# Weight buffers moved by 96 bytes against x and the activated tiles

## The chip, the cores and the metric

One Trainium2 chip, one core. The time is device microseconds of one execution of the whole kernel. A core has five engines that run side by side: TensorE (PE, with its weight loads shown as PEld), VectorE (DVE), ScalarE (ACT), GpSimd (POOL) and SyncE (SP, which issues most transfers). SBUF is the on-chip memory of 128 partitions; an address below is a byte offset within each partition.

## The reference

One inference step of a one-layer decoder trunk on 256 prompt tokens and 8 x 4 sample tokens (288 in all, width 2048). Each sub-layer stands between two RMS norms:

```
x = x + 0.5 * norm1(swiglu(norm0(x), ffn1_w_in, ffn1_w_out))      # hidden width 5632
x = x + norm3(hybrid_mixer(norm2(x), mix_w_in, ..., mix_w_out))   # two groups of gated linear recurrences
x = x + 0.5 * norm5(swiglu(norm4(x), ffn2_w_in, ffn2_w_out))

def swiglu(x, w_in, w_out):
    gate, up = split(x @ w_in, 2)
    return (silu(gate) * up) @ w_out
```

All is float32. Outputs are x for prompt and sample and the new recurrent states.

## The kernel before

Activations are kept transposed: the 2048 features as 16 tiles of 128 partitions x 288 tokens. To keep float32 accuracy with one-pass matmuls, each operand is split into a high part (rounded to the matmul's float32r) and a low part (what is left). A product of a weight block and an activation tile is three matmuls into the same PSUM tile, high x high, high x low and low x high (lines 615 to 617). The weights are the stationary operand, loaded anew before each matmul, and the 288 tokens stream past:

```
yield lambda: PE.matmul(dst, w[0][:, a, c], parts[0], ...)   # L615: high weights, high x
yield lambda: PE.matmul(dst, w[0][:, a, c], parts[1], ...)   # L616: high weights, low x
yield lambda: PE.matmul(dst, w[1][:, a, c], parts[0], ...)   # L617: low weights, high x
```

Weights arrive in units of 256 x 512 numbers (two k tiles, four column blocks of 128). `Weights.load` has SP fetch one into a raw tile (3 buffers of 4096 bytes); `Weights.pieces` splits it: ACT writes the high half (L119), DVE the low half (L120) of a tile `wh` of 8192 bytes, in which each of the two k tiles has 512 high numbers and behind them 512 low ones. `wh` has 4 buffers in the pool hlp, and for about a third of the units around each border between sub-layers 2 extra buffers in a pool hx on the right side of SBUF. Every unit feeds 24 matmuls. `block` walks over units, column blocks and k tiles; the order is that of the code.

The high and low parts of an activation tile lie in one tile of 2304 bytes. `pair` allots it as four places of 576 bytes; each place holds 72 high numbers, then 72 low ones, so a low part starts 288 bytes behind its high part. A matmul reads 4 numbers (16 bytes) from each of the four places in turn, then the next 4 (`turns_of`):

```
PLACES, LINE = 4, 4
t = pool.tile([P, PLACES, 2, T // PLACES], F32R, name=name)
return t[:, :, 0, :], t[:, :, 1, :]
def turns_of(t):
    return t.rearrange("p g (i e) -> p i g e", e=LINE)
```

Such tiles are xp (x, 16 tiles), fill x and y (4 + 4 tiles at each border, in a pool `fl`), and hp (the activated hidden tiles silu(gate) * up, 2 buffers in the pool ffn, each four tiles in the same layout).

Pools on the left of SBUF are stacked upward in the order in which they are opened: const, xpool (x, y, xp, rt, rp, acc, cols), rawp, hlp (the four wh), sqp, colp, then the pools of the sub-layer (ffn1, mixer or ffn2). Pools on the right are stacked downward: a pool `top` with a gap of 224 bytes, hx below it, fl below that. Within a pool the first tile has the lowest address. Before the change, modulo 128: every wh is at 0, the high part of every xp, hp and fill tile at 64, the low part at 64 + 288 = 96. So wh stands 64 bytes past a high part and 32 past a low part, in all products.

Of the kernel before, what the change touches and what calls it, by code (L numbers as in the profile page):

```python
# [9 lines left out]
F32 = mybir.dt.float32  # L10
# [6 lines left out]
P = 128  # L17
# [31 lines left out]
def pair(pool, name):  # L49

    t = pool.tile([P, PLACES, 2, T // PLACES], F32R, name=name)
    return t[:, :, 0, :], t[:, :, 1, :]
# [97 lines left out]
def trunk_kernel(ctx, tc, x_prompt, x_sample, state_gla, state_hgrn, norm_gains, f1_in, f1_out, f2_in, f2_out,  # L150
# [6 lines left out]
    xpool = ctx.enter_context(tc.tile_pool(name="xpool", bufs=1))  # L157
    rawp = ctx.enter_context(tc.tile_pool(name="rawp", bufs=RAW_BUFS))
    hlp = ctx.enter_context(tc.tile_pool(name="hlp", bufs=HL_BUFS))
    mmp = ctx.enter_context(tc.tile_pool(name="mmp", bufs=5, space=PSUM))  # L160
    aux = ctx.enter_context(tc.tile_pool(name="aux", bufs=3, space=PSUM))
    sqp = ctx.enter_context(tc.tile_pool(name="sqp", bufs=2))
# [63 lines left out]
    def wider(n):  # L226

        return {i for i in range(n - 44, n + 4) if i // 2 % 3 == (n + 2) // 2 % 3}
# [268 lines left out]
    class PreNorm:  # L497
# [3 lines left out]
        def __init__(self, name, update, ahead, at):  # L501

            self.name, self.update, self.ahead, self.at, self.late = name, update, ahead, at, []
            self.tmps = None
# [25 lines left out]
    class Fill:  # L530
# [2 lines left out]

        def __init__(self, pool, name, gains, gnext, some, ahead):
            self.gnext, self.name, self.some, self.ahead = gnext, name, some, ahead

            self.tiles = [[pair(pool, f"{name}{n}{k}") for k in range(EARLY)] for n in "xy"]
            self.gains = pool.tile([P, 48], F32, name=f"{name}g")[:, 0:EARLY]
            V.tensor_tensor(self.gains, gains[:, 0:EARLY], prm[:, gnext * KT:gnext * KT + EARLY], op=ALU.mult)
# [138 lines left out]
    def ffn(tag, gcol, gnext, pn, before, fill=None):  # L678
# [2 lines left out]
        border = []  # L681
        with ExitStack() as pools:
            fp = pools.enter_context(tc.tile_pool(name=f"ffn{tag}", bufs=2))
            hid, final_tiles = {}, []

            def do_in(c):
# [1008 lines left out]
    class Border:  # L1695


        def __init__(self, n, gains, gnext, some, ahead=0):
            self.pools = ExitStack()
            top = self.pools.enter_context(tc.tile_pool(name=f"top{gnext}", bufs=1, side="right"))  # L1700
            top.tile([P, 56], F32, name=f"gap{gnext}")
            W.begin_extra(self.pools.enter_context(tc.tile_pool(name=f"hx{gnext}", bufs=2, side="right")), wider(n))
            self.fill = Fill(self.pools.enter_context(tc.tile_pool(name=f"fl{gnext}", bufs=1, side="right")),
                             f"fill{gnext}", gains, gnext, some, ahead)

    pn = pre1 = PreNorm("pre1", x_first, FIRST, 11)
    pn.late.append(prm2)
    u, border = ffn(1, lambda k: hg1[:, k:k + 1], 2, pn, first)
    u, border = mixer(PreNorm("pre2", u, UPDATED, 11), border)
    ffn(2, lambda k: hg1[:, KT + k:KT + k + 1], None, PreNorm("pre3", u, UPDATED, 11), border.pools, border.fill)  # L1710


# [39 lines left out]
```

## Time and profile before

| | |
|---|---|
| runs | median 2184.03 us (2183.36 to 2198.98) of 3 |
| profiled execution | 2185.01 us, span 2183.2 us, granted TensorE clock 0.999 |
| TensorE matmuls | 17828, busy 2174.0 us |
| weight loads | 17828, busy 2155.0 us |
| VectorE, ScalarE | busy 1384.0 and 1018.5 us |
| read from HBM | 363.75 MB, 172 GB/s with what is written |

The span is the time from the first to the last instruction. Matmuls are pipelined: one is recorded as some 290 ns long, while the next starts after about 130 ns. So the distance from start to start is what a matmul costs, and it is got by counting records in a window of time.

### The profile page before, as it was taken

The numbers are of one execution on the slowest core, as the hardware profiler recorded it, in microseconds if no ns is written. First come the engines' busy times: TensorE is split into PE (matmuls) and PEld (weight loads), VectorE is DVE, ScalarE is ACT, GpSimd is POOL, SyncE is SP. The second block draws the span as 40 slices with busy tenths as digits, with TensorE's granted clock in tenths as the row PEclk, the third lists the DMA queues.
The fourth block names the chain that finished last, engine by engine and source line by source line (L and its number), as shares of the span: only waits on it lengthen the run. The fifth ranks groups of instructions, "written<-read, shape, count | busy, mean of one in ns | idle before, by whom it ended". The sixth has DMA issues, their size and how long they took to land.

```text
span 2183.2 us, 43224 instructions
## 1 busy us (share of the span) xinstructions
PE 2174.0 (100%) x17828; PEld 2155.0 (99%) x17828; DVE 1384.0 (63%) x2253; ACT 1018.5 (47%) x1537; POOL 180.0 (8%) x327
## 2 busy tenths in 40 slices
PE   9999999999999999999999999999999999999999
PEld 9999999999999999999999999999999999999998
DVE  7655546554656468888898756745555466556656
ACT  6453434343334346665677654543334343433344
POOL 2000000000000001323300000000000020122005
PEclk9999999999999999999999999999999999999999
DMA  7655555555556554677665664655655565666555
GB/s 220 182 173 173 173 174 172 174 173 174 174 174 192 167 172 136 202 214 207 178 187 170 183 195 126 181 167 164 175 173 167 172 178 175 177 179 184 167 168 160
DMA packets 227335, 384.87 MB, mean 176 GB/s; under 512 B 21363, under 2 KB 60865, under 8 KB 227137
## 3 DMA queue, kind: packets, MB, share of 16 engines
q1 hardware_dynamic: 213872, 365.02, 56.1%
q0 software_dynamic: 10992, 16.77, 2.8%
q8 instruction: 140, 2.29, 0.4%
q10 hardware_dynamic: 2272, 0.31, 0.1%
q14 instruction: 59, 0.48, 0.1%
HBM read 363.75 MB, written 11.80 MB: 172 GB/s over the span
## 4 chain that ended last, share of the span: by engine, by line
PE 92%; DVE 3%; DMA 2%; ACT 1%; issue 1%; SPq 0%; POOL 0%; ACTq 0%; DVEq 0%; POOLq 0%
PE gate L616 10%; PE gate L615 9%; PE gate L617 9%; PE out L616 8%; PE out L615 8%; PE up L616 8%; PE out L617 8%; PE up L615 8%; PE up L617 8%; PE mo L616 2%; PE mo L615 2%; PE mo L617 2%; PE hfq L615 1%; PE hfq L616 1%; PE hfq L617 1%; DVE wh L120 1%
## 5 line engine op out<-in xcount | busy, mean ns | idle before, releaser
L120 DVE TENSOR_TENSOR wh<-raw,wh 128x1024 fp32r<-128x1024 f32 (+1 forms) x676 | 821.6, 1217 | 597.5 <-ACT wh L119 595.8
L119 ACT ACTIVATE wh<-raw 128x1024 fp32r<-128x1024 f32 (+1 forms) x676 | 710.3, 1052 | 923.9 <-PE gate L617 289.0
L615 PE MATMUL gate<-xp,wh 128*128 128x288 f32 x1660 | 481.9, 292 | 0.2
L616 PE MATMUL gate<-xp,wh 128*128 128x288 f32 x1660 | 480.8, 292 | 0.5 <-DVE xp L282 0.4
L617 PE MATMUL gate<-xp,wh 128*128 128x288 f32 x1660 | 477.9, 289 | 0.0
L616 PE MATMUL out<-hp,wh 128*128 128x288 f32 x1408 | 410.6, 292 | 0.0
L616 PE MATMUL up<-xp,wh 128*128 128x288 f32 x1408 | 410.5, 292 | 0.0
L615 PE MATMUL out<-hp,wh 128*128 128x288 f32 x1408 | 409.0, 290 | 0.3 <-DVE y L801 0.3
L615 PE MATMUL up<-xp,wh 128*128 128x288 f32 x1408 | 408.9, 290 | 0.0
L617 PE MATMUL out<-hp,wh 128*128 128x288 f32 x1408 | 407.6, 289 | 0.0
L617 PE MATMUL up<-xp,wh 128*128 128x288 f32 x1408 | 407.1, 289 | 0.0
L615 PEld LDWEIGHTS gate<-xp,wh 128*128 128x128 f32 x1660 | 311.2, 188 | 1.1 <-issue 0.3
L616 PEld LDWEIGHTS gate<-xp,wh 128*128 128x128 f32 x1660 | 310.2, 188 | 1.6 <-DVE xp L282 1.3
L617 PEld LDWEIGHTS gate<-xp,wh 128*128 128x128 f32 x1660 | 311.1, 188 | 0.2 <-DVE wh L120 0.2
L615 PEld LDWEIGHTS out<-hp,wh 128*128 128x128 f32 x1408 | 264.6, 188 | 0.6 <-DVE y L801 0.5
L615 PEld LDWEIGHTS up<-xp,wh 128*128 128x128 f32 x1408 | 264.3, 188 | 0.0
L617 PEld LDWEIGHTS up<-xp,wh 128*128 128x128 f32 x1408 | 264.2, 188 | 0.1
L617 PEld LDWEIGHTS out<-hp,wh 128*128 128x128 f32 x1408 | 264.3, 188 | 0.0
L616 PEld LDWEIGHTS out<-hp,wh 128*128 128x128 f32 x1408 | 264.0, 188 | 0.0
L616 PEld LDWEIGHTS up<-xp,wh 128*128 128x128 f32 x1408 | 264.0, 188 | 0.0
L801 DVE TENSOR_TENSOR y<-out,y 128x288 f32<-128x288 f32 x287 | 119.7, 452 | 79.2 <-PE out L617 78.7
L758 POOL DMA_DIRECT2D xT<-b x64 | 37.1, 586 | 754.8 <-PE gate L617 564.8
(417 smaller groups left out, 2549.0 us busy)
## 6 DMA issues: line engine op xcount, KB each, us to landing
raw<-in_ffn_w_in_dram SPq DMA_DIRECT2D x350, 512.0 KB, 3.7
raw<-in_ffn_w_out_dram SPq DMA_DIRECT2D x176, 512.0 KB, 3.6
raw<-in_mix_w_in_dram SPq DMA_DIRECT2D x64, 512.0 KB, 4.3
raw<-in_mix_w_in_dram SPq DMA_DIRECT2D x96, 256.0 KB, 3.4
raw<-in_mix_w_out_dram SPq DMA_DIRECT2D x32, 512.0 KB, 3.7
out_dram<-s POOLq DMA_DIRECT2D x32, 256.0 KB, 2.9
s<-in_state_gla_dram SPq DMA_DIRECT2D x16, 256.0 KB, 5.6
s<-in_state_hgrn_dram SPq DMA_DIRECT2D x16, 256.0 KB, 5.6
```

Of the source, the lines that this page charges most:

```text
L119: i1 = self.nc.scalar.activation(h[:, a, c], raw[:, a, c], AF.Copy).ins
L120: i2 = self.nc.vector.tensor_tensor(l[:, a, c], raw[:, a, c], h[:, a, c].bitcast(F32), op=ALU.subtract).ins
L615: yield lambda: PE.matmul(dst, w[0][:, a, c], parts[0], start=start, stop=False)
L616: yield lambda: PE.matmul(dst, w[0][:, a, c], parts[1], start=False, stop=False)
L617: yield lambda: PE.matmul(dst, w[1][:, a, c], parts[0], start=False, stop=stop)
L758: queues[n % len(queues)].dma_start(dst[q * TS:(q + 1) * TS, 4 * g:4 * g + 4, :, cols].rearrange("p k t c -> p (k t) c"), b32[rows, q])
L801: V.tensor_tensor(y[k], ps, y[k], op=ALU.add)
```

## The change

Three gaps are added and one is made larger; nothing else is changed. A tile that is only allotted takes space and no time.

```
     hlp = ctx.enter_context(tc.tile_pool(name="hlp", bufs=HL_BUFS))
+    hlp.tile([P, 24], F32, name="gap_w", bufs=1)
...
         def __init__(self, pool, name, gains, gnext, some, ahead):      # class Fill
             self.gnext, self.name, self.some, self.ahead = gnext, name, some, ahead
+            pool.tile([P, 24], F32, name=f"{name}gap")
...
             fp = pools.enter_context(tc.tile_pool(name=f"ffn{tag}", bufs=2))
+            fp.tile([P, 8], F32, name=f"gap_f{tag}", bufs=1)
...
             top = self.pools.enter_context(tc.tile_pool(name=f"top{gnext}", bufs=1, side="right"))
-            top.tile([P, 56], F32, name=f"gap{gnext}")
+            top.tile([P, 64], F32, name=f"gap{gnext}")
```

The line numbers 615 to 617 become 617 to 619, and 119 and 120 stay.

More of the change, by code (lines that the diff above doesn't have):

```diff
@@ L159, in trunk_kernel @@
     hlp = ctx.enter_context(tc.tile_pool(name="hlp", bufs=HL_BUFS))
+    hlp.tile([P, 24], F32, name="gap_w", bufs=1)
     mmp = ctx.enter_context(tc.tile_pool(name="mmp", bufs=5, space=PSUM))
@@ L535, in __init__ @@
             self.gnext, self.name, self.some, self.ahead = gnext, name, some, ahead
+            pool.tile([P, 24], F32, name=f"{name}gap")
             self.tiles = [[pair(pool, f"{name}{n}{k}") for k in range(EARLY)] for n in "xy"]
@@ L683, in ffn @@
             fp = pools.enter_context(tc.tile_pool(name=f"ffn{tag}", bufs=2))
+            fp.tile([P, 8], F32, name=f"gap_f{tag}", bufs=1)
             hid, final_tiles = {}, []
@@ L1700, in __init__ @@
             top = self.pools.enter_context(tc.tile_pool(name=f"top{gnext}", bufs=1, side="right"))
-            top.tile([P, 56], F32, name=f"gap{gnext}")
+            top.tile([P, 64], F32, name=f"gap{gnext}")
             W.begin_extra(self.pools.enter_context(tc.tile_pool(name=f"hx{gnext}", bufs=2, side="right")), wider(n))
```

## The prediction

> **What bounds the kernel now.** I read the page first: which engine is busy, at which clock, and what the chain that ended last is made of.
>
> ```profile
> span 2183.2 us, 43224 instructions
> PE 2174.0 (100%) x17828; PEld 2155.0 (99%) x17828; DVE 1384.0 (63%) x2253; ACT 1018.5 (47%) x1537; POOL 180.0 (8%) x327
> PEclk9999999999999999999999999999999999999999
> PE 92%; DVE 3%; DMA 2%; ACT 1%; issue 1%; SPq 0%; POOL 0%; ACTq 0%; DVEq 0%; POOLq 0%
> ```
>
> TensorE's matmuls and its weight loads both fill the whole span, the clock is never withheld, and 92% of the last chain is matmuls of the three product lines. Next, the waits of TensorE alone, the longest three:
>
> ```profile
> PE warm L330 <- POOL onesD L252: 1.1, 1, 1.1
> PE o L1364 <- DMA Vh<-y: 0.7, 1, 0.7
> PE sc L1117 <- DVE k_g L1180: 0.5, 1, 0.5
> ```
>
> So in 2183 us TensorE waits for others a few us in all. No transfer, no split of weights and no evacuation of results sets the time; only how often a product can start does. A record of 0.29 us says little of that, since records overlap. The timeline shows it by the starts:
>
> ```profile
> 400.00 0.29 PE L615 MATMUL up<-xp,wh 128*128 128x288 f32 x1
> 400.13 0.29 PE L616 MATMUL up<-xp,wh 128*128 128x288 f32 x1
> 400.26 0.29 PE L617 MATMUL up<-xp,wh 128*128 128x288 f32 x1
> 400.38 0.29 PE L615 MATMUL up<-xp,wh 128*128 128x288 f32 x1
> ```
>
> Three products, L615 (high weights, high x), L616 (high weights, low x), L617 (low weights, high x), take 0.38 us from start to start, 0.127 us each. To see it over the span I count records in windows of TensorE (length, busy time, count):
>
> ```profile
> 64.00:691.00 627.00, 626.98 (x4950) 1.00 0.58 175
> 701.00:815.00 114.00, 113.78 (x875) 1.00 0.57 175
> 1208.00:1339.00 131.00, 131.00 (x1012) 1.00 0.61 184
> 1402.00:2164.00 762.00, 761.85 (x5878) 1.00 0.59 173
> ```
>
> A record is longer than two starts are apart, so about two records of a window began before it. 627 us / 4948 = 126.7 ns per product; 114 / 873 = 130.6 (130.3 without the 0.22 us idle); 131 / 1010 = 129.7; 762 / 5876 = 129.7. **This is the row that matters most.** The same instruction on the same kind of tiles has two rhythms, one of 126.7 ns for the first 627 us and one near 129.7 ns for nearly all the rest, and inside a window nothing interrupts it. Neither the clock (1.00 in all four) nor the DMA share (0.57 to 0.61) tells the windows apart. Nor do the addresses: in both, weights stand 64 bytes past the high x and 32 past the low x, modulo 128. So distance cannot be all that sets the gap; a rhythm is entered at a restart after a short stop and then kept.
>
> How many products there are follows from the transfers that feed them:
>
> ```profile
> raw<-in_ffn_w_in_dram SPq DMA_DIRECT2D x350, 512.0 KB, 3.7
> raw<-in_ffn_w_out_dram SPq DMA_DIRECT2D x176, 512.0 KB, 3.6
> raw<-in_mix_w_in_dram SPq DMA_DIRECT2D x64, 512.0 KB, 4.3
> raw<-in_mix_w_in_dram SPq DMA_DIRECT2D x96, 256.0 KB, 3.4
> raw<-in_mix_w_out_dram SPq DMA_DIRECT2D x32, 512.0 KB, 3.7
> ```
>
> 350 + 176 + 64 + 96/2 + 32 = 670 units, and 2 more that the start loads by rows, 672. Each has 2 k tiles x 4 column blocks x 3 products = 24, so 16,128, and the borders add 24: 16,152 products, 5,384 of each line. One ns on every product is 16.2 us, 0.74% of the time. 4,950 of them run in the fast rhythm and about 11,200 near 129.7.
>
> The profiled execution took 2185.01 us, 1.8 us more than its span, and the median of the runs is 2184.03. The highest of them is 2198.98. If its first 627 us had run at 129.7 instead of 126.7, it would be 4950 x 3.0 ns = 14.9 us longer than the median, 2198.9. That fits, though only the profiled run has a trace.
>
> **The change part by part.** It adds and removes no instruction, wait or transfer, and leaves the order on every engine as it is. It moves addresses, worked out here from tile sizes and the order of pools. Ahead of the weight buffers stand 96 more bytes, so they begin at 96 instead of 0 modulo 128. The next gap of 32 bytes brings hp back to where it was (96 + 32 = 128). On the right side the gap grows from 224 to 256 bytes, and since pools there grow downward, the two extra weight buffers move by -32, which is 96 modulo 128 too. x parts stay at 64 (high) and 96 (low). Hence:
>
> - L615 and L617 (high x): distance 64 before, 32 after.
> - L616 (low x): distance 32 before, 0 after.
> - The gap in the fill pool is its first tile, below the fill tiles, so these move with the extra buffers and keep 64 and 32. That is 48 of 16,152 products: nothing.
>
> Mixer tiles (gp, cst, tmp), sq, nh and rc move too. They are read by DVE, ACT and by small matmuls. DVE is at 63% and ACT at 47%, and TensorE waits some us for them in all; that slack covers any change there, and if it did not, the three waits above are the places to look. I put this at nothing.
>
> So the sum is the gap of three kinds of products at new distances. What do the rows say of distance? The nearest is the difference between the lines inside one rhythm, first 100 to 600 us, then 1450 to 1950 (busy, mean ns):
>
> ```profile
> L616 PE MATMUL gate<-xp,wh 128*128 128x288 f32 x448 | 129.7, 290 | 0.0
> L615 PE MATMUL gate<-xp,wh 128*128 128x288 f32 x448 | 129.0, 288 | 0.0
> L617 PE MATMUL gate<-xp,wh 128*128 128x288 f32 x448 | 128.5, 287 | 0.0
> ...
> L616 PE MATMUL gate<-xp,wh 128*128 128x288 f32 x448 | 131.5, 293 | 0.0
> L615 PE MATMUL gate<-xp,wh 128*128 128x288 f32 x448 | 130.9, 292 | 0.0
> L617 PE MATMUL gate<-xp,wh 128*128 128x288 f32 x448 | 130.1, 290 | 0.0
> ```
>
> Record lengths follow the gaps: they rise by 3 to 4 ns from the fast to the slow rhythm, as the gap does (3.0). L616, the only line at distance 32, is longer than the mean of the two at 64 by 290 - 287.5 = 2.5 ns and by 293 - 291 = 2.0 ns. I take 2.25.
>
> - Two lines go from 64 to 32. At the price of L616 that is +2.25 ns each: 2 x 5,384 x 2.25 = **+24 us**. From below: if the excess of L616 belongs to the line (its place in the triple) and not to the distance, nothing, or a gain that takes both lines to the shortest record (below). I take the +24 because it is the only row at distance 32.
> - L616 goes to distance 0, which no row shows. A moving tile is read in runs of 16 bytes from four places 576 bytes apart, so each turn alternates between two positions 64 bytes apart modulo 128. At distance 0 the reader therefore visits the same two positions as at 64, in the other order. By that, L616 becomes as short as the others, 5,384 x -2.25 = **-12 us**.
>
> The ends for it are the shortest and longest records of undisturbed products (min/median/max):
>
> ```profile
> L616 PE MATMUL up<-xp,wh x1408: 288/291/300, 35.9 to 2119.7; 128*128 128x288 f32 x176
> ...
> L617 PE MATMUL up<-xp,wh x1408: 286/288/382, 36.0 to 2119.9; 128*128 128x288 f32 x176
> ```
>
> If L616 went to 286, 291.5 - 286 = 5.5 ns less, -30 us; to 300, +8.5 ns, +46 us. I take -12, the value by symmetry, which lies between.
>
> **Sum:** +24 - 12 = +12 us on 2184.0, **2196 us**, 0.5% slower (2197 for an execution like the profiled one). The bounds: upward 24 + 46 = +70, 2254. Downward, all three lines at 286 (L615, L617 and L616 by 2, 1 and 4 ns for the 4,950 products of the fast rhythm, by 6, 4 and 7 ns for the rest): 1650 x 7 + 3734 x 17 ns = 75 us, 2109.
>
> A rule of the Trainium skill speaks against any effect: TensorE: Matmul & The Clock Gate, section "Step-by-step: what each phase is for", says that the engine has two independent read ports, one for the moving operand and one for weight loads, so "Loading the next tile's weights doesn't steal SBUF read bandwidth from the running matmul." By that the sum is 0. The same page, section "Wait — 56ns, not 53.3ns?", gives a warm gap of N / 2.4 GHz plus about 2.5 ns, which for 288 columns is 122.5 ns as an estimate; the trace has 126.7 and 129.7, so here something costs 4 to 7 ns more, and by how much differs between windows.
>
> **Rivals.**
>
> *The distance has no say.* The gap comes from rhythms that a restart picks. For it: two rhythms at the same distances. Against: L616 is longer in both. Time: 2184, and 2199 when the first window falls into the slow rhythm as well. The change would then not do what its distances suggest, though the addresses do move. It is the outcome by the rule of the Trainium skill named above (TensorE: Matmul & The Clock Gate).
>
> *Faster.* At 32 and 0 the weight load and the moving reads miss each other better, and products run at 126.7 or less wherever they run 129.7 now: 11,200 x 3.0 = 34 us, 2150; towards 2109 if all are like the shortest. For it: 126.7 is held undisturbed for 627 us, so the slow rhythm is not needed by anything; the supply keeps up with it (PE busy 626.98 of 627.00). Against: no row at distance 32 is shorter.
>
> *Slower.* At distance 0 the low x and the next weights begin on the same place modulo 128 and walk into each other. Place: L616 of every triple. Price: up to +46 us beside the +24, 2254. It decides from where L616 merely stays as long as it is: then +24 stands alone, 2208, 1.1% slower. For it: single L616 records of 300 ns exist at today's distances. Against: the 64-byte alternation, by which 0 and 64 are alike.
>
> **How the numbers follow.** The forecast, distance prices of about 2 ns either way, 0.30, with its own range 2180 to 2206 for the choice of rhythms. No say: 0.14. Faster by its mechanism: 0.26. Slower by its mechanism: 0.30. A change of under 1% cannot be told from none here, which is about 22 us. Same takes the first two cases less 0.01: 0.43; faster 0.26; slower 0.31. The range must leave out no more than 2 in 10: I cut the third of the faster case that lies under 2140 and the third of the slower case above 2235, so 2140 to 2235.
>
> **What the profile afterwards would show.** Same counts and same order, TensorE at 100%, waits of some us. The windows' counts give the gaps: forecast 127.5 to 130.5 ns. Record lengths of L615 and L617 should rise by 2 ns in the same rhythm and L616 fall to theirs; if L616 stays longest whatever its distance, the excess was the line's. If windows still fall into 126.7 and 129.7, distance has no say. One new rhythm over the whole span, below 126 or above 131, would make my sum wrong: then a distance sets the rhythm, and single-line differences were no guide.

## The result and the profile after

Eleven runs of each: median 2178.35 us after (2177.24 to 2180.41), 2196.50 us before. The ratio, taken of the means, is 0.9934, with a 95% interval of 0.9914 to 0.9954: 0.66% faster, where 0.5% slower was forecast. The time lies in the stated range and within 1% of the forecast, but the kernel moved the other way. In the experiments below, one run of e2 (2386.54 us at a granted clock of 0.85) and one of e6 (2589.94 us at 0.78) are slow runs and count in no ratio, nor do, beside e2 to e4 and e9 to e12, the runs of before that lie more than 1.5% above the fastest of them.

The two kernels differ in spread too. After, all runs lie within 3.2 us. Before, four of eleven lie at 2183.4 to 2185.8 and seven at 2195.9 to 2199.6. The 2184.03 from which the prediction worked is the lower group; the profiled execution (2185.01) belongs to it.

The page of after, its span and engines:

```profile
span 2176.5 us, 43224 instructions
PE 2166.9 (100%) x17828; PEld 2148.0 (99%) x17828; DVE 1384.1 (64%) x2253; ACT 1017.8 (47%) x1537; POOL 180.1 (8%) x327
```

The same work, and TensorE is full as before. The waits of TensorE, the longest:

```profile
PE warm L331 <- POOL onesD L253: 1.1, 1, 1.1
PE sc L1120 <- DVE k_g L1183: 1.0, 2, 0.6
```

No wait is longer than about a microsecond, as before. So the time went in the gap from product to product. Windows of TensorE after (length, busy, count), alternately gate and up blocks, which read xp, and out blocks, which read hp:

```profile
64.00:106.00 42.00, 42.00 (x332) 1.00 0.63 185
108.00:133.00 25.00, 25.00 (x196) 1.00 0.56 166
136.00:180.00 44.00, 44.00 (x347) 1.00 0.58 172
181.00:205.00 24.00, 24.00 (x188) 1.00 0.57 172
208.00:254.00 46.00, 46.00 (x364) 1.00 0.58 172
```

With two records off for the edges: gate and up 127.3, 127.5 and 127.1 ns, out 128.9 and 129.0. From the undisturbed starts (the next product starts within 150 ns) it is 127.42 ns in a gate and up block and 129.2 in an out block (129.1 over all out blocks), from the first chunk to the last, save near the borders. In the two FFN parts of before, one rhythm ran through gate, up and out alike and changed only at stops. Now the rhythm changes with the block, in the same way each time, and the runs agree. Over all undisturbed products the mean start-to-start distance went from 128.54 ns in the first trace to 128.08, times 15,940 is 7.3 us, against 6.7 us between the two spans. The rest of the 18 us between the medians is the distance between the two groups of before. Most runs of before lie in the upper group and the profiled one did not; that the upper group has the slow rhythm in ffn1 too is an inference, as no run of it has a trace.

The lines inside the new rhythm, gate blocks of after, 1450 to 1950 us (busy, mean ns):

```profile
L617 PE MATMUL gate<-xp,wh 128*128 128x288 f32 x448 | 129.8, 290 | 0.0
L618 PE MATMUL gate<-xp,wh 128*128 128x288 f32 x448 | 129.4, 289 | 0.0
L619 PE MATMUL gate<-xp,wh 128*128 128x288 f32 x448 | 129.4, 289 | 0.0
```

The second line is no longer the longest, and the first and third, which have the same distance, differ.

### The profile page after: what moved, and what is told of

The parts are those of the page before. It is cut to its first block, busy times and chain, and to the rows that moved or that the text cites. A ratio compares the mean times of both kernels' runs of the same rounds, so it can differ in the third digit from the quotient of the medians.

```text
span 2176.5 us, 43224 instructions
## 1 busy us (share of the span) xinstructions
PE 2166.9 (100%) x17828; PEld 2148.0 (99%) x17828; DVE 1384.1 (64%) x2253; ACT 1017.8 (47%) x1537; POOL 180.1 (8%) x327
## 4 chain that ended last, share of the span: by engine, by line
PE 93%; DVE 3%; DMA 2%; ACT 1%; issue 1%; POOL 0%; ACTq 0%; DVEq 0%; POOLq 0%
PE gate L617 9%; PE gate L618 9%; PE gate L619 9%; PE out L619 8%; PE out L618 8%; PE out L617 8%; PE up L619 8%; PE up L618 8%; PE up L617 8%; PE hfq L617 1%; PE hfq L618 1%; PE hfq L619 1%; PE mo L617 1%; PE mo L619 1%; PE mo L618 1%; DVE wh L120 1%
## 5 line engine op out<-in xcount | busy, mean ns | idle before, releaser
L617 PE MATMUL gate<-xp,wh 128*128 128x288 f32 x1660 | 481.2, 291 | 0.5 <-DVE u L713 0.3
L619 PE MATMUL gate<-xp,wh 128*128 128x288 f32 x1660 | 477.5, 289 | 0.0
L617 PE MATMUL out<-hp,wh 128*128 128x288 f32 x1408 | 410.9, 292 | 0.0
L619 PE MATMUL out<-hp,wh 128*128 128x288 f32 x1408 | 409.3, 291 | 0.0
L617 PE MATMUL up<-xp,wh 128*128 128x288 f32 x1408 | 408.1, 290 | 0.0
L619 PE MATMUL up<-xp,wh 128*128 128x288 f32 x1408 | 406.4, 289 | 0.0
L617 PEld LDWEIGHTS gate<-xp,wh 128*128 128x128 f32 x1660 | 310.6, 187 | 1.4 <-issue 0.5
L619 PEld LDWEIGHTS gate<-xp,wh 128*128 128x128 f32 x1660 | 310.8, 188 | 0.2 <-DVE wh L120 0.2
L619 PEld LDWEIGHTS out<-hp,wh 128*128 128x128 f32 x1408 | 265.5, 189 | 0.0
L617 PEld LDWEIGHTS out<-hp,wh 128*128 128x128 f32 x1408 | 263.9, 187 | 0.3 <-DVE y L804 0.3
L619 PEld LDWEIGHTS up<-xp,wh 128*128 128x128 f32 x1408 | 264.0, 187 | 0.0
L617 PEld LDWEIGHTS up<-xp,wh 128*128 128x128 f32 x1408 | 263.7, 187 | 0.0
```

The costliest lines, as they stand in the source:

```text
L617: yield lambda: PE.matmul(dst, w[0][:, a, c], parts[0], start=start, stop=False)
L619: yield lambda: PE.matmul(dst, w[1][:, a, c], parts[0], start=False, stop=stop)
```

## The experiments

In the new trace gate and up on one side and out on the other have the same distances modulo 128. They differ modulo 256: the weights went up by 96 bytes, hp by 128, xp not at all. So weights stand 32 past the high part of xp, but 160 past that of hp. Hence the theory M256: the gap goes by the distance between weights and activated tile modulo 256 (or a multiple). Its rival M128 lets modulo 128 decide. The last blocks of ffn1 in the same trace already speak for M256. A third of their units lie in the two extra buffers, which went down by 32 bytes and so stand 160 past the high part of xp and 32 past that of hp. From their starts, gate and up take 128.0 ns there and out 128.6: in each case a third of the way from the one value to the other, though modulo 128 nothing differs.

The experiments ran on three chips (e1 to e4, e5 to e8, e9 to e12). The runs of before beside them fall into groups at the same times on all three (the shortest group was not met beside e5 to e8), so medians are compared across them. Ratios are not: they hang on how many runs of before fell into which group.

**e1, the kernel before, profiled again.** Is a rhythm drawn at a restart, at unchanged addresses?

> The unchanged kernel, profiled once more. Theory R (a restart draws the rhythm, at the same addresses): if the time is near 2197.5, the window 64 to 691 us holds about 4840 product records (129.7 ns each) instead of 4950, and all else is as in the first profile; if it is near 2184, the window holds about 4950 again. Rival S (something else than the products is longer in the long executions): the window holds about 4950 whatever the time.

It took 2179.70 us, which neither case had named. Its windows:

```profile
64.00:811.00 747.00, 747.00 (x5899) 1.00 0.58 176
1399.00:2159.00 760.00, 760.00 (x5865) 1.00 0.58 173
```

747 us / 5897 = 126.7 ns and 760 / 5863 = 129.6. In the first profile the fast rhythm ended between 695 and 701 us: one product came 66 ns late, and 5 us later TensorE sat idle for 0.32 us until DVE had written y. In e1 it did not stop there (it was busy for all of the 11 us from 691 to 702), and the fast rhythm went on to 811. Some 890 products more at 126.7 instead of 130.0 are 2.9 us, and some in the mixer too; the execution is 5.3 us shorter. The instructions and addresses are the same, so they do not settle how long a rhythm lasts; in these two traces it lasts until TensorE stops. Whether the same stop can lead to different rhythms they do not show, since both have 126.7 ns first and 129.6 in ffn2, so neither R nor S is decided. In 66 further runs of the kernel before, beside the experiments, times lie in three groups: 2163 to 2167 (5 runs), 2179 to 2185, and 2193 to 2201. The first would fit the fast rhythm in both FFN parts and the last the slow one in both; no run of either has a trace.

**e2, hp at the same place as xp modulo 256.** The changed kernel with

```
-            fp.tile([P, 8], F32, name=f"gap_f{tag}", bufs=1)
+            fp.tile([P, 40], F32, name=f"gap_f{tag}", bufs=1)
```

> The changed kernel, with the gap ahead of hp 128 bytes larger, so that hp stands where xp stands modulo 256 (distance to the weights 32 high, 0 low, as with xp; modulo 128 nothing moves). Theory M256 (the gap goes by the distance modulo 256 or more): the out blocks, now near 129.1 ns, run at 127.4 ns as gate and up do; 4200 products x 1.7 ns = 7 us less, 2171 us. Rival M128 (modulo 128 decides, and out blocks are slower for another reason): nothing changes, 2178 us and 129.1 ns in the out blocks.

Median 2170.45 us, 7.9 less than after; against before 0.9943 (0.9910 to 0.9975), an interval made wide by the groups of before. Its windows, an out block, a gate and up block, and ffn2:

```profile
108.00:133.00 25.00, 25.00 (x199) 1.00 0.56 171
136.00:180.00 44.00, 44.00 (x348) 1.00 0.57 171
1401.00:2149.00 748.00, 748.00 (x5873) 1.00 0.59 176
```

The out block now holds 199 records in the same 25 us instead of 196, and ffn2 as a whole runs at 748 / 5871 = 127.4 ns. Modulo 128 nothing had moved. M128 falls; the 96 + 32 = 128 of the change, meant to put hp back, cost 8 us.

**e3, the same 128 bytes in the kernel before.**

```
             fp = pools.enter_context(tc.tile_pool(name=f"ffn{tag}", bufs=2))
+            fp.tile([P, 32], F32, name=f"gap_f{tag}", bufs=1)
```

> The kernel before, with 128 bytes ahead of hp and nothing else moved: all distances modulo 128 stay (64 high, 32 low), but the out blocks differ from gate and up modulo 256. M256: out blocks have another gap than gate and up, and as block follows block the rhythm is broken each time, so the executions agree within 3 us instead of falling into 2184 and 2197.5. M128: as before, both 2184 and 2197.5 are met and out blocks run as gate and up.

Median 2191.27 us, ratio 1.0034 (0.9993 to 1.0076), unclear. Runs spread over 2185.1 to 2196.4, so the agreement within 3 us that M256 expected is not there. The windows (out, gate and up, out, gate and up, gate and up):

```profile
108.00:132.00 24.00, 24.00 (x188) 1.00 0.54 170
134.00:181.00 47.00, 47.00 (x365) 1.00 0.56 170
182.00:207.00 25.00, 25.00 (x196) 1.00 0.56 170
209.00:254.00 45.00, 45.00 (x357) 1.00 0.58 175
...
1552.00:1598.00 46.00, 46.00 (x357) 1.00 0.57 169
```

Out blocks stay near 129.0 ns by these counts (129.4 from all their undisturbed starts); gate and up run at 47 / 363 = 129.5 and 45 / 355 = 126.8 in turn, chunk after chunk. So an out block at another distance breaks the rhythm each time, as M256 says, and gate and up fall into the one or the other of their two. That they do so almost strictly in turn was not expected.

**e4, one distance modulo 256 for all.** Of the kernel before, with the fill tiles and the two extra weight buffers moved as well:

```
+    hlp.tile([P, 24], F32, name="gap_w", bufs=1)
+            fp.tile([P, 40], F32, name=f"gap_f{tag}", bufs=1)
-            top.tile([P, 56], F32, name=f"gap{gnext}")
+            top.tile([P, 96], F32, name=f"gap{gnext}")
+            pool.tile([P, 24], F32, name=f"{name}gap")      # in Fill, behind the fill tiles
```

> Weights at +96 bytes against all activated tiles modulo 256: as e2, and the two extra weight buffers and the fill tiles too are put at the same place modulo 256 (32 high, 0 low for every product). M256: every product runs at 127.4 ns; against e2 it gains where the extra buffers are used (a third of 44 units at each border, about 700 products x 1.7 ns = 1 us), 2170 us. M128: as after, 2178 us.

Median 2169.18 us, ratio 0.9941 (0.9906 to 0.9976). Both FFN parts:

```profile
64.00:699.00 635.00, 635.00 (x4986) 1.00 0.58 174
1372.00:2148.00 776.00, 775.66 (x6088) 1.00 0.59 176
```

635 / 4984 = 127.4 and 775.7 / 6086 = 127.4: one rhythm, past every stop. The whole gain over after is 9.2 us. The 1.3 us of it that go beyond e2 belong to the extra buffers and fill tiles, but they are less than the 3.3 us over which the runs of e4 spread.

**e5, the activations move instead.** Is it the distance, or the weights' own place? The weights stay at 0 modulo 256.

```
+    xpool.tile([P, 40], F32, name="gap_x")                   # ahead of xp
+    xpool.tile([P, 24], F32, name="gap_r")                   # behind cols
+            fp.tile([P, 40], F32, name=f"gap_f{tag}", bufs=1)
+            pool.tile([P, 24], F32, name=f"{name}gap")       # in Fill, behind the fill tiles
```

> Weights stay where they are before the change (0 modulo 256); xp, hp and fill tiles move instead, by 160 bytes, so that weights stand 32 past every high part and 0 past every low part modulo 256, as in e4. Theory M256, distance between the two: one rhythm of 127.41 ns over the whole span as in e4, 2169 us. Rival A256, the weights' own place modulo 256 (0 before, 96 in e4): as before the change, rhythms of 126.67 and 129.63 ns, 2180 to 2198 us.

Median 2169.39 us, as e4 to 0.2 us; the ratio of 0.9900 (0.9861 to 0.9939) differs from e4's 0.9941 because the runs of before beside it fell into their groups in other shares:

```profile
65.00:694.00 629.00, 629.00 (x4939) 1.00 0.58 174
1401.00:2149.00 748.00, 748.00 (x5873) 1.00 0.59 176
```

127.4 ns in both. The distance decides; the weights' place by itself does not. This drops A256.

**e6 to e11, the other distances modulo 256**, uniform for all products as in e4 (shift s: gap_w of s bytes, gap_f of 256 - s, the gap of `top` larger by 256 - s, the gap in Fill s):

```
+    hlp.tile([P, s // 4], F32, name="gap_w", bufs=1)         # s = 128, 64, 32, 224, 160, 192
```

> Weights at +128 against all activated tiles modulo 256, uniform as in e4. Modulo 128 this is the kernel before (64 high, 32 low). M256: the rhythm is that of the out blocks of e3, which have this distance, 129.4 ns, everywhere, some 0.8 ns over the first profile of before, so 2197 us and no spread of 15 us. Rival M128: rhythms of 126.67 and 129.63 ns, executions in two groups.

> Weights at +64 against all activated tiles modulo 256 (128 and 96 past the high and low parts' places before; now 0 past high, 224 past low). Not seen in any trace so far. M256 expects one set of rhythms for the whole span, of its own, between 125 and 131 ns (2140 to 2225 us), gate, up and out alike. Rival (the gain of e4 comes from leaving the distance of before, whatever the new one): 127.4 ns, 2169 us.

> Weights at +32 against all activated tiles modulo 256 (224 past high, 192 past low). Not seen so far. M256: a set of rhythms of its own, between 125 and 131 ns (2140 to 2225 us), gate, up and out alike. Rival (the gain of e4 comes from leaving the distance of before, whatever the new one): 127.4 ns, 2169 us.

> Weights at +224 modulo 256 against all activated tiles (160 past high, 128 past low): the distance that the out blocks have in the changed kernel. Modulo 128 it is the same as e4. M256: out blocks keep the 129.1 ns they have there and gate and up join them, so e6's time less 0.26 ns on 16,152 products, 2188 to 2196 us. Rival M128: as e4, 127.41 ns and 2169 us.

> Weights at +160 modulo 256 (96 past high, 64 past low). Not seen in any trace. M256: rhythms of its own, the same in gate, up and out, between 125 and 131 ns; modulo 128 it is the same as e8 (128.9 to 130.5 ns, 2194.7 us), so M128 expects 2195 us and M256 a time more than 3 us off that.

> Weights at +192 modulo 256 (128 past high, 96 past low). Not seen in any trace. Modulo 128 it is the same as e7 (127.78 ns, 2173.4 us), so M128 expects 2173 us and M256 a time more than 3 us off that, with a gap between 125 and 131 ns.

Windows of TensorE, e6:

```profile
65.00:690.00 625.00, 625.00 (x4831) 1.00 0.57 171
1410.00:2160.00 750.00, 749.80 (x5793) 1.00 0.58 173
```

e7:

```profile
64.00:690.00 626.00, 626.00 (x4902) 1.00 0.57 173
1405.00:2150.00 745.00, 745.00 (x5833) 1.00 0.59 175
```

e8:

```profile
64.00:825.00 761.00, 760.97 (x5902) 1.00 0.57 173
1410.00:2160.00 750.00, 749.79 (x5739) 1.00 0.58 172
```

e9, with a window of the output projection in between:

```profile
65.00:690.00 625.00, 625.00 (x4839) 1.00 0.57 171
1220.00:1355.00 135.00, 135.00 (x1015) 1.00 0.60 179
1420.00:2160.00 740.00, 740.00 (x5729) 1.00 0.58 174
```

e10:

```profile
64.00:825.00 761.00, 760.39 (x5899) 1.00 0.57 173
1412.00:2168.00 756.00, 756.00 (x5867) 1.00 0.58 174
```

e11:

```profile
64.00:812.00 748.00, 747.74 (x5903) 1.00 0.58 176
1394.00:2138.00 744.00, 744.00 (x5876) 1.00 0.59 177
```

Time divided by count less two gives the gaps; beside them the medians and the ratios to before:

| weights past the high part, modulo 256 (128) | gaps in the traces, ns | median, us | ratio (95%) |
|---|---|---|---|
| 0 (0), e7 | 127.8 | 2173.43 | 0.9917 (0.9887 to 0.9947) |
| 32 (32), e4 | 127.4 | 2169.18 | 0.9941 (0.9906 to 0.9976) |
| 64 (64), e6 | 129.4 | 2196.60 | 1.0026 (0.9999 to 1.0054) |
| 96 (96), e10 | 128.9 | 2182.68 | 0.9984 (0.9947 to 1.0022) |
| 128 (0), e11 | 126.7 | 2159.45 | 0.9863 (0.9813 to 0.9914) |
| 160 (32), e9 | 129.2, 133.3 | 2197.84 | 1.0049 (1.0016 to 1.0082) |
| 192 (64), before | 126.7, 129.6, 130.0 | 2196.50 | |
| 224 (96), e8 | 129.0, 130.7 | 2194.68 | 1.0028 (0.9999 to 1.0057) |

Every pair that is the same modulo 128 (0 and 128, 32 and 160, 96 and 224) is 12 to 29 us apart, so M128 is out; 64 and 192 have like medians, but in the traces one of them has one rhythm and the other three. e6 came out at the 2197 us that M256 had from the out blocks of e3. e9 was foretold at 2188 to 2196 from the out blocks of after and came 2 us above. In its trace the output projection fell into a slower rhythm of 133.3 ns that no trace had shown; its 768 products at 4.1 ns more are 3 us. Rivals that saw the gain in merely leaving the old distance fall with e6, e8 and e9. The runs of e10 spread over 2176 to 2191, so it too may have more than one rhythm; its only trace, of an execution of 2188.95, shows one.

e11 beats both kernels: 18.9 us less than after. It holds 126.7 ns in both FFN parts, also past the stop at 700 us; all four runs lie within 2158.7 to 2160.5. The mean is that of the fast rhythm of before, but here products follow each other every 126 or 127 ns, while there the distances go from 124 to 129. The lines in its gate blocks:

```profile
L617 PE MATMUL gate<-xp,wh 128*128 128x288 f32 x448 | 129.0, 288 | 0.0
L618 PE MATMUL gate<-xp,wh 128*128 128x288 f32 x448 | 129.0, 288 | 0.0
L619 PE MATMUL gate<-xp,wh 128*128 128x288 f32 x448 | 128.8, 288 | 0.0
```

**e12, the order of reading.** e4 with the same start addresses, but a moving tile read in runs of 72 numbers:

```
 def turns_of(t):
-    return t.rearrange("p g (i e) -> p i g e", e=LINE)
+    return t
```

> e4, but each matmul reads its moving tile, and writes PSUM, in runs of 72 numbers per place instead of 4 from each of the four places in turn. Same start addresses, same distances, same products. Theory C (the gap above 120 ns is what the reads of the moving tile and of the next weights cost each other on their way, so the order of reading counts as much as the start): another gap than 127.41 ns, by more than 0.5 ns, either way. Rival F (a fixed cost of each matmul that the start addresses alone set): 127.41 ns and 2169 us.

Median 2237.99 us, ratio 1.0243 (1.0172 to 1.0314):

```profile
65.00:719.00 654.00, 654.00 (x4990) 1.00 0.57 170
723.00:840.00 117.00, 117.00 (x880) 1.00 0.55 170
1435.00:2205.00 770.00, 770.00 (x5875) 1.00 0.57 171
```

131.1 ns, and 133.3 in the middle; the trace is of the shortest of four runs (2225.82 to 2251.94). So rival F falls: start addresses alone do not set the gap, and the order of the numbers counts as much (3.7 ns here, 4.0 between e11 and the slow part of e8). Theory C is not shown by it. The edit changes the order of reading and that of writing to PSUM together, and they are not told apart here.

## Why the prediction was wrong, and where it was right

*What bounds the kernel* was right: what lies outside the undisturbed products is between 126 and 136 us in every trace, and the rest of each span is the number of products times their gap.

*The rhythms* were read rightly in the FFN parts. In the mixer, v, hi and hfq had means of 128.0 to 128.9 ns, not near 129.7. That a rhythm is kept from stop to stop is what e1 shows; that a restart draws it is argued from the groups of times alone. But I took the draw as a margin of the forecast and three runs as the base. More runs put the median of before at 2196.50, 12.5 us higher, in the slower group. After, all runs lie within 3.2 us. Most of the 18 us lies here.

*The +24 us* failed, and with it the direction. The step priced a distance by the difference between L616 and the other two lines inside one rhythm. But the three lines share one rhythm, which may repeat only after several triples, and the length of a line's record does not follow its own distance. After, L617 and L619 at one distance are 290 and 289; in e11 lines at 128, 96 and 128 are all 288. The rows of before could have warned: L615 and L617 had the same distance and differed by 1 and 2 ns, nearly the 2.25 that I took from L616. Besides, the end of a matmul's record is modelled by the profile; starts are the better measure. What the distances did instead is to set the whole rhythm: 127.42 ns in gate and up, 129.2 in out. Over all products that is 0.46 ns less than in the first trace, 7.3 us off where this step and the next had put 12 us on.

*The -12 us by symmetry* failed in the symmetry itself, and with its modulus. I argued that distances 64 bytes apart visit the same two positions modulo 128 in the other order. But distances even 128 apart differ by up to 29 us (32 and 160). Modulo 256 the four places stand 0, 64, 128 and 192 bytes on, so by the same argument distances of 0, 64 and 128 would be alike; they have 127.8, 129.4 and 126.7 ns (e7, e6, e11). So the same positions in another order are not the same gap. The measure is modulo 256 at least; whether 512 would matter, these runs cannot tell, since xp tiles are 2304 bytes apart, so both halves of 512 occur in every pair of k tiles.

That 2196 still lies within 1% of 2178.35 is luck: the sum of the steps had the wrong sign, and it is small beside the time.

*"Brings hp back to where it was"* failed with the modulus. It is the term that the change itself got wrong, and e2 prices it at 7.9 us.

*Mixer tiles, DVE and ACT at nothing* held: e4 and e5 move different tiles and agree to 0.2 us. The fill tiles were never moved by themselves.

*The rivals.* "Distance has no say" falls with e4, e5 and e11. That was the outcome by the rule of the Trainium skill (TensorE: Matmul & The Clock Gate, "Step-by-step: what each phase is for"), that loading the next weights takes no SBUF read bandwidth from the running matmul. Measured here, start addresses alone move the gap from 126.7 (e11) to 130.7 ns (e8), so the rule does not give this kernel's time; what it is that waits, no run shows. "Faster" was closest, and its end of 2150 is near the 2159.45 of e11, but at its own distances, 32 and 0, products take 127.4 ns, not 126.7 or less, and in the change only gate and up have them. "Slower at distance 0" was wrong: where the weights start at the place of the low part (e4) or of the high part (e7), modulo 256, the kernel is among the fastest.

Open: which part of the chip makes 256 bytes the measure; why some distances have one rhythm and others three; and whether other distances between the high and the low part would do better still. None of these was tried.

## What to carry to other kernels

Where TensorE is full and waits for nothing, count records per window: a start-to-start distance that changes in steps at stops, with the same instructions, is a rhythm, and three runs are too few to place the median among its levels. Relative places of the stationary and the moving tile are then worth a sweep over a whole period (here 256 bytes in steps of 32, worth 1.8% from best to worst), with every pool that feeds products moved to the same distance. A difference between neighbouring lines in one rhythm prices nothing.

## What the runs showed of the hardware

The same three float32 matmuls of 288 columns cost 126.7 to 133.3 ns each, by start addresses, order of reading or writing, and history. In most traces the rhythms are sharp. Averaged over hundreds to thousands of undisturbed starts they are 126.67, 127.41, 127.78, 128.89, 129.63, 130.00, 131.11 and 133.33 ns, which makes nine products 1140, 1146.7, 1150, 1160, 1166.7, 1170, 1180 and 1200 ns, all multiples of 3.33 ns. A repeat over nine products, three triples, is also what the starts show, to about 1 ns, in the 129.6 ns rhythm of before; its fast rhythm repeats over six. The 129.4 ns of e6, the 129.2 ns of e9 and the 130.7 ns of e8 are means of longer patterns (12, 21 and 15 products) and stand outside this list. What steps in 3.33 ns was not measured by itself.
